# Rotary position in the retention heads: partners 64 features apart, sines multiplied across partitions on two engines

## The chip, the core and the metric

The kernel runs on one core of one Trainium2 chip. The metric is the device time of one execution in microseconds, of which the median of three is taken. The profile that is read here is one more execution, taken by the hardware profiler. TensorE (PE) does the matrix products, VectorE (DVE), ScalarE (ACT) and GpSimd (POOL) the elementwise work, and SyncE (SP) and ScalarE issue the transfers. Each engine works through its own instructions in the order in which the program lists them. An instruction that waits for another engine holds up all that stand behind it in its own queue.

## What is computed

One block of a diffusion transformer over 2048 tokens of 1024 features: a modulated norm, a mixer with four HGRN2 heads and four retention heads of 128 features each, an output projection, and a convolutional feed-forward part. The change touches the rotary position of the retention heads' queries and keys, before they enter the chunked retention scan. Cut to that:

```python
def _rope_2d(t, rows, cols):
    half = t.shape[-1] // 2
    quarter = half // 2
    freqs = ROPE_THETA ** (-jnp.arange(quarter, dtype=jnp.float32) / quarter)

    def rot(u, pos):
        ang = pos[:, None] * freqs[None, :]
        cos, sin = jnp.cos(ang), jnp.sin(ang)
        u1, u2 = u[..., :quarter], u[..., quarter:]
        return jnp.concatenate([u1 * cos - u2 * sin, u1 * sin + u2 * cos], axis=-1)

    return jnp.concatenate([rot(t[..., :half], rows), rot(t[..., half:], cols)], axis=-1)
...
    rq = _heads(rq, RET_HEADS)
    rk = _heads(rk, RET_HEADS) * (RET_DK ** -0.5)
    rv = _heads(rv, RET_HEADS)
    if pos is not None:
        rq = _rope_2d(rq, pos[0], pos[1])
        rk = _rope_2d(rk, pos[0], pos[1])
...
    def step(r, inp):
        qc, kc, vc = inp
        scores = jnp.einsum('bhtk,bhsk->bhts', qc, kc) * intra
        o = (jnp.einsum('bhts,bhsv->bhtv', scores, vc)
             + jnp.einsum('bhtk,bhkv->bhtv', qc * q_dec[:, :, None], r))
        r_new = (chunk_dec[:, None, None] * r
                 + jnp.einsum('bhsk,bhsv->bhkv', kc * k_dec[:, :, None], vc))
        return r_new, o
```

Each feature is multiplied by a cosine, and its partner, 32 features further on or back, by a sine with a sign; the two are added. The products of queries with keys do not depend on the order of a head's 128 features, as long as both have the same.

## The kernel before

The heads come one after the other, first the four HGRN2 heads, then the four retention heads, and each goes over the 2048 tokens in four groups of 512. While PE, DVE and ACT work on the scan of one group, the projections of the next are woven between (`weave`, `step`): `ret_proj` makes queries, keys and values of a group, `ret_sweep1` uses them a group later, and `ret_sweep2` and `ret_sweep2b` finish the group of the head before. There are thus 16 runs of `ret_proj`, four heads by four groups; they are called units 1 to 16 here, in order of time. They lie between about 740 and 1290 us of the span.

In `ret_proj` a tile `qk` holds queries and keys of the group, 128 features on the partitions and 2 x 512 tokens along each. It is written in pieces out of PSUM by DVE (L587) and last by ACT (L585, in the helper `scaled`), and it has the slots named K0 and K1, so that the profile shows it as K. A second tile of the same size, `pt`, shows as Q. Four transfers that ACT issues (L1169) copy `qk` into `pt` with blocks of 32 partitions swapped in pairs. GpSimd multiplies `pt` by the sines (L1189), DVE multiplies `qk` by the cosines in place (L1192) and adds `pt` to it (L1193). Between the copies and these lies the projection of values and gates (in the fourth head of values alone). The cosines' product is held back until the last combining addition of that projection (`issue_after`). The first to use the rotated tile is PE, with the products of keys and queries (L1202, `rsc`).

Three other chains run on the same queues. The norm of a finished group: ACT sums squares (L913), GpSimd makes the reciprocal root in six small steps (L67 to L72, `rstd`), DVE scales by it (L935, or L1243 in retention heads), and PE transposes the result (L920, `otp`). The rotary tables are loaded for each group by ACT's queue (L1159, cosines into a single buffer, sines into one of three). And the weights and the modulation are prepared a head ahead (L291, L489 to L498, L644, L645).

The order on every queue is set by a scheduler that goes by its own model of durations when the program is built. A change in what stands in `ret_proj` can therefore move its neighbours as well.

Of the kernel before, what the change touches and what calls it, by code (L numbers as in the profile page):

```python
# [15 lines left out]
ALU = mybir.AluOpType  # L16
PSUM = bass.MemoryType.PSUM

P = 128
# [3 lines left out]
G = 512  # L23
# [6 lines left out]
NIN = 4608  # L30
# [11 lines left out]
H = G // 2  # L42
RING = 10
SEQUENCE = 0, 1, 5, 6, 4, 3, 2


def view(t, off, dims):
    return bass.AP(t.tensor, t.offset + off, [t.ap[0]] + dims)


class Kern:
# [411 lines left out]

    def features(self, h, g, ms=SEQUENCE):

        if g in self.X:
            return self.X.pop(g)
        X = [None] * 7
        for m in ms:
            X[m] = self.slot_tile([P, 4, 2, H], F16, "hx", "hx")  # L470
            self.nc.sync.dma_start(X[m], self.hxd[g][m])
        return X
# [679 lines left out]
    def ret_proj(self, pool, h, g, W, pr, cur):  # L1152
        nc = self.nc
        X = self.features(NH + h, g)
        qk, pt = self.kq_tiles()
        cos = pool.tile([P, G], F32, tag="Ta", bufs=1, name="cos")
        sin = pool.tile([P, G], F32, tag="Kl", bufs=KL, name="sin")
        for i, r in enumerate((cos, sin)):
            nc.scalar.dma_start(r, self.I["rope"][:, i, g * G:(g + 1) * G])  # L1159
        w, dq = W["z"]  # L1160
        if "dqk" not in W:
            W["dqk"] = self.kp.tile([P, 1], F32, tag="dqk", bufs=2, name="dqk")
            nc.vector.tensor_scalar(W["dqk"], dq, P ** -0.5, None, ALU.mult)

        def kq(f, half, c, s):
            self.scaled(qk[:, 1 - f, half * H:(half + 1) * H], c, s, dq if f else W["dqk"])
        yield from self.head_unit(*self.fm(w, X, H), kq, (W["dqk"], dq))
        for b in range(4):
            nc.scalar.dma_start(pt[32 * b:32 * b + 32], qk[32 * (b ^ 1):32 * (b ^ 1) + 32])  # L1169
        V = pool.tile([P, 4, P], F32, tag="V", bufs=2, name="rV")  # L1170
        if h < NH - 1:
            w, dqv = W["vg"]
            gate = self.gate_tile().rearrange("p (c t) -> p c t", t=P)

            def vg(f, half, c, s):
                cs = slice(2 * half, 2 * half + 2)
                if f:
                    c = self.whole(c, s)
                    nc.scalar.activation(gate[:, cs], c, AF.Silu, scale=dqv)
                else:  # L1180
                    self.scaled(V[:, cs], c, s, dqv)
            yield from self.head_unit(*self.tm(w, X, H), vg, (dqv, None))
            self.silu_bound(h, g, gate)
            cur["sg"][g] = gate
        else:
            w, dqv = W["v"]
            yield from self.single(*self.tm(w, X, H), dqv, lambda half: V[:, 2 * half:2 * half + 2])

        nc.gpsimd.tensor_tensor(pt, pt, view(sin, 0, [[0, 2], [1, G]]), ALU.mult)  # L1189

        with self.tc.issue_after(self.last.ins):
            nc.vector.tensor_tensor(qk, qk, view(cos, 0, [[0, 2], [1, G]]), ALU.mult)  # L1192
        nc.vector.tensor_tensor(qk, qk, pt, ALU.add)  # L1193
        pr.update(qk=qk, V=V)
# [596 lines left out]
def _consts():  # L1791
    s = np.arange(P)
    masks = []
    for h in LEVELS:
        same = (s[:, None] // (2 * h)) == (s[None, :] // (2 * h))
        m = (same & ((s[:, None] // h) != (s[None, :] // h))).astype(np.float32)
        if 2 * h <= B:
            masks.append(np.concatenate([m[j:j + B, j:j + B] for j in range(0, P, B)], 0))
    masks = np.concatenate(masks, 1)
    f = s.astype(np.float32)  # L1800
    ramp = np.zeros((P, 4, P), np.float32)
    rel = f[None, :] - f[:, None]
    ramp[:, 0], ramp[:, 1] = np.maximum(rel, 0), np.maximum(-rel, 0)
    ramp[:, 2], ramp[:, 3] = rel >= 0, rel <= 0
    colr = np.stack([P - 1 - f, f, f + 1, P - f], 1).astype(np.float32)
    fr = (np.float32(10000.0) ** (-np.arange(32, dtype=np.float32) / np.float32(32))).astype(np.float32)
    pos = np.arange(64, dtype=np.float32)
    ang = (fr[s % 32][:, None] * pos[None, :]).astype(np.float32)
    sign = np.where((s % 64) < 32, -1.0, 1.0).astype(np.float32)

    tok = np.arange(SEQ)
    at = np.where((s < 64)[:, None], ang[:, tok // 64], ang[:, tok % 64])
    rope = np.stack([np.cos(at), np.sin(at) * sign[:, None]], 1).astype(np.float32)
    return dict(ident=np.eye(P, dtype=np.float32), masks=masks, ramp=ramp, colr=colr, rope=rope)

# [21 lines left out]
```

## Time and profile before

| | |
|---|---|
| three runs | 2725.51 us median (2723.41 to 2730.9) |
| the profiled execution | 2735.92 us, of it span 2734.1 us |
| PE busy | 2557.4 us, 94% of the span |
| DVE busy | 1821.8 us, 67% |
| ACT busy | 1343.0 us, 49% |
| POOL busy | 779.3 us, 29% |
| PE's mean granted clock | 0.969 of full speed |

Times inside the span are counted from its start. A gap is the time that an engine sat idle just before an instruction, and its releaser the instruction that ended the wait. PE is the busiest engine by far, so what counts is where PE sits idle and which chain of other engines it waits for there. A busy PE instruction takes longer at a lower granted clock, so gaps and clock have to be read together.

### The profile page before, as it was taken

Reading aid. Unit: us, or ns where it says so; the run is one execution under the profiler, and the core shown is the slowest. Engines: PE = TensorE matmul, PEld = TensorE weight load, DVE = VectorE, ACT = ScalarE, POOL = GpSimd, SP = SyncE. Lnnn points to the kernel's source line nnn. Section 1 sums busy time; section 2 is a strip of 40 time slices with the busy share of each in tenths; the row PEclk is TensorE's granted clock in tenths of the full one; section 3 lists DMA queues with packets and bytes.
Section 4 is the critical chain, followed back from the end, with each engine's and each line's share of the span. In section 5 each row is a group of like instructions: output and inputs, shape, how many; then the busy total and the mean of one; then the engine's idle time right before and its main releaser. Section 6 shows DMA issues by size and latency. Waiting matters only on the chain.

```text
span 2734.1 us, 56424 instructions
## 1 busy us (share of the span) xinstructions
PE 2557.4 (94%) x22829; PEld 1686.3 (62%) x22829; DVE 1821.8 (67%) x3569; ACT 1343.0 (49%) x2902; POOL 779.3 (29%) x905
## 2 busy tenths in 40 slices
PE   5788999999999999988999899999999999999998
PEld 2578888889888888887445344444444444444443
DVE  4988677776757565546464888877877777423553
ACT  4776456564544444435454566555555554411120
POOL 3733112220313132221244344334433433000101
PEclk6799999999999999999999999999999999999999
DMA  8224334243447676766631133333233234734552
GB/s 282 115 86 156 103 110 135 93 132 115 144 132 255 207 238 198 241 184 196 211 110 62 57 121 104 108 112 113 99 105 116 89 112 163 268 143 172 205 194 100
DMA packets 216694, 402.39 MB, mean 147 GB/s; under 512 B 16623, under 2 KB 98771, under 8 KB 211824
## 3 DMA queue, kind: packets, MB, share of 16 engines
q1 hardware_dynamic: 203808, 373.42, 39.8%
q10 hardware_dynamic: 12320, 25.18, 3.0%
q8 instruction: 179, 2.93, 0.4%
q14 instruction: 83, 0.68, 0.1%
q0 software_dynamic: 304, 0.17, 0.0%
HBM read 298.57 MB, written 91.75 MB: 143 GB/s over the span
## 4 chain that ended last, share of the span: by engine, by line
PE 61%; DVE 15%; DMA 8%; issue 7%; ACT 4%; POOL 4%; ACTq 1%; SPq 0%; POOLq 0%; DVEq 0%
PE pa L84 6%; PE pa L85 6%; PE pa L86 6%; PE pd L86 5%; PE pd L84 5%; PE pd L85 5%; DMA Q<-K 3%; PE pc L84 3%; PE pc L85 3%; PE pc L86 3%; PE pb L84 2%; PE pb L86 2%; PE pb L85 2%; PE opp L84 2%; PE opp L85 2%
## 5 line engine op out<-in xcount | busy, mean ns | idle before, releaser
L84 PE MATMUL pa<-feat,w 128*128 128x512 f16 x704 | 268.4, 381 | 14.2 <-ACT ta L545 9.8
L85 PE MATMUL pa<-feat,w 128*128 128x512 f16 x704 | 268.1, 381 | 0.0
L86 PE MATMUL pa<-feat,w 128*128 128x512 f16 x704 | 264.9, 381 | 0.0
L86 PE MATMUL pd<-wd,actl 128*128 128x512 f16 x616 | 233.5, 379 | 0.0
L85 PE MATMUL pd<-wd,actl 128*128 128x512 f16 x616 | 233.5, 379 | 0.0
L84 PE MATMUL pd<-wd,actl 128*128 128x512 f16 x616 | 232.8, 379 | 0.0
L85 PEld LDWEIGHTS <-w 128*128 128x128 f16 x1232 | 120.7, 98 | 156.8 <-issue 16.9
L86 PEld LDWEIGHTS <-w 128*128 128x128 f16 x1232 | 121.4, 99 | 145.3 <-issue 1.7
L84 PEld LDWEIGHTS <-w 128*128 128x128 f16 x1232 | 121.5, 99 | 141.4 <-issue 2.0
L85 PEld LDWEIGHTS <-hx 128*128 128x128 f16 x1824 | 182.0, 100 | 9.5 <-issue 7.3
L86 PEld LDWEIGHTS <-hx 128*128 128x128 f16 x1824 | 182.1, 100 | 2.8 <-issue 1.9
L84 PEld LDWEIGHTS <-hx 128*128 128x128 f16 x1824 | 182.4, 100 | 2.3
L1593 DVE SCALAR_TENSOR_TENSOR st<-act,modT,st 128x512 f16<-128x512 f32 x154 | 144.3, 967 | 32.1 <-ACT st L1592 32.1
L1592 ACT ACTIVATE st<-act,modT 128x512 f16<-128x512 f32 x154 | 107.3, 718 | 85.2 <-DVE act L1582 31.4
L84 PE MATMUL pa<-w_vg,hx 128*128 128x128 f16 x800 | 145.2, 222 | 2.9 <-DVE cb L579 2.3
L85 PE MATMUL pa<-w_vg,hx 128*128 128x128 f16 x800 | 144.9, 222 | 0.0
L86 PE MATMUL pa<-w_vg,hx 128*128 128x128 f16 x800 | 144.8, 222 | 0.0
L84 PE MATMUL pc<-feat,w 128*128 128x512 f16 x352 | 133.5, 379 | 1.2 <-ACT feat L1367 1.1
L86 PE MATMUL pc<-feat,w 128*128 128x512 f16 x352 | 133.5, 379 | 0.0
L85 PE MATMUL pc<-feat,w 128*128 128x512 f16 x352 | 133.5, 379 | 0.0
L84 PE MATMUL pa<-hx,w_z 128*128 128x256 f16 x464 | 127.7, 275 | 5.1 <-ACT ct L545 1.6
L85 PEld LDWEIGHTS <-w_z 128*128 128x128 f16 x1072 | 109.2, 102 | 36.4 <-issue 24.1
(550 smaller groups left out, 7563.0 us busy)
## 6 DMA issues: line engine op xcount, KB each, us to landing
hx<-hxd SPq DMA_DIRECT2D x212, 512.0 KB, 4.9
actd<-st SPq DMA_DIRECT2D x154, 256.0 KB, 2.0
actl<-actd SPq DMA_DIRECT2D x28, 1024.0 KB, 5.0
wur<-in_w_up_dram SPq DMA_DIRECT2D x44, 512.0 KB, 3.8
raw<-in_w_in_dram SPq DMA_DIRECT2D x36, 512.0 KB, 4.3
wm<-in_w_mod_dram SPq DMA_DIRECT2D x64, 256.0 KB, 3.8
hxd<-hx SPq DMA_DIRECT2D x28, 512.0 KB, 3.2
wdb<-in_w_down_dram SPq DMA_DIRECT2D x44, 256.0 KB, 4.0
```

The costliest lines, as they stand in the source:

```text
L84: mm(ps, lhs(0), rhs(0), start=start, stop=False, skip_group_check=True)
L85: mm(ps, lhs(0), rhs(1), start=False, stop=False, skip_group_check=True)
L86: mm(ps, lhs(1), rhs(0), start=False, stop=stop, skip_group_check=True)
L1592: nc.scalar.activation(p[:, 0], v, AF.Copy, scale=s)
L1593: nc.vector.scalar_tensor_tensor(p[:, 1], v, s, p[:, 0], ALU.mult, ALU.subtract)
```

## The change

The two columns of weights that make queries and keys of a retention head are put in another order on the way into the kernel, so that the partner of feature p lies at p + 64 or p - 64, and no longer 32 away in blocks. The cosine and sine tables are put in the same order. The four copies go. Instead GpSimd multiplies the lower 64 partitions of `qk` by the sines and writes the product to the upper 64 partitions of `pt`, and DVE does the other half, from the upper partitions to the lower. Both stand right behind the pieces of `qk`, before the projection of values and gates; GpSimd's product behind that projection goes. The sign of a sine now goes with the partition that is read. Cosines and addition stay as they were.

```diff
+HALVES = np.arange(P).reshape(2, 2, 32).transpose(1, 0, 2).reshape(P)
...
         yield from self.head_unit(*self.fm(w, X, H), kq, (W["dqk"], dq))
-        for b in range(4):
-            nc.scalar.dma_start(pt[32 * b:32 * b + 32], qk[32 * (b ^ 1):32 * (b ^ 1) + 32])
+        sines = view(sin, 0, [[0, 2], [1, G]])
+        nc.gpsimd.tensor_tensor(pt[64:], qk[:64], sines[:64], ALU.mult)
+        nc.vector.tensor_tensor(pt[:64], qk[64:], sines[64:], ALU.mult)
         V = pool.tile([P, 4, P], F32, tag="V", bufs=2, name="rV")
...
-        nc.gpsimd.tensor_tensor(pt, pt, view(sin, 0, [[0, 2], [1, G]]), ALU.mult)
         with self.tc.issue_after(self.last.ins):
             nc.vector.tensor_tensor(qk, qk, view(cos, 0, [[0, 2], [1, G]]), ALU.mult)
...
-    sign = np.where((s % 64) < 32, -1.0, 1.0).astype(np.float32)
+    sign = np.where(s < 64, 1.0, -1.0).astype(np.float32)
...
-    at = np.where((s < 64)[:, None], ang[:, tok // 64], ang[:, tok % 64])
+    at = np.where((HALVES < 64)[:, None], ang[HALVES][:, tok // 64], ang[HALVES][:, tok % 64])
...
+    order = np.arange(NIN)
+    for o in range(2560, 3584, P):
+        order[o:o + P] = o + HALVES
+    named["w_in"] = np.ascontiguousarray(named["w_in"][:, :, order])
```

The lines behind the change are four to six higher than before. Outside the retention heads and the first steps of the output projection the queues' order is as it was.

GpSimd's queue at units 3 and 4, whose two products stand next to each other ahead of a norm's six steps (L67 to L72, after: L71 to L76; raw is a weight tile). Before:

```order
L489 TENSOR_TENSOR raw<-raw 128x512
L492 TENSOR_TENSOR raw<-raw 128x512
L495 TENSOR_TENSOR raw<-raw 128x512
L498 TENSOR_TENSOR raw<-raw 128x512
L1189 TENSOR_TENSOR Q<-Q,sin 128x1024 x2
L67 TENSOR_SCALAR rs_v<-ossq 128x4
L68 TENSOR_TENSOR rs_y<-rs_v,mhalf 128x4
```

After:

```order
L493 TENSOR_TENSOR raw<-raw 128x512
L496 TENSOR_TENSOR raw<-raw 128x512
L499 TENSOR_TENSOR raw<-raw 128x512
L502 TENSOR_TENSOR raw<-raw 128x512
L1174 TENSOR_TENSOR Q<-K,sin 64x1024 x2
L71 TENSOR_SCALAR rs_v<-ossq 128x4
L72 TENSOR_TENSOR rs_y<-rs_v,mhalf 128x4
```

Nothing moved: the products stand in the same places, but read K in place of Q, and so wait for the pieces of `qk` and no longer for a transfer.

VectorE's queue at unit 7, from the last piece of `qk` that DVE writes (K<-pc) to a piece of the values (rV); w_z is a weight tile, modT the modulation. Before:

```order
L587 SCALAR_TENSOR_TENSOR K<-pc,dq,ct 128x256
L645 SCALAR_TENSOR_TENSOR w_z<-raw,p2s,w_z 128x512 x2
L235 TENSOR_TENSOR modT<-modt_ps,sv 128x4
L645 SCALAR_TENSOR_TENSOR w_z<-raw,p2s,w_z 128x512
L587 SCALAR_TENSOR_TENSOR rV<-pb,dq,ct 128x256
```

After:

```order
L591 SCALAR_TENSOR_TENSOR K<-pc,dq,ct 128x256
L649 SCALAR_TENSOR_TENSOR w_z<-raw,p2s,w_z 128x512 x2
L239 TENSOR_TENSOR modT<-modt_ps,sv 128x4
L1175 TENSOR_TENSOR Q<-K,sin 64x1024
L649 SCALAR_TENSOR_TENSOR w_z<-raw,p2s,w_z 128x512
L591 SCALAR_TENSOR_TENSOR rV<-pb,dq,ct 128x256
```

One instruction came in between weights that are being prepared; the rest kept its order.

VectorE's queue at unit 13, the first of the last head, from a group's state (Kt, Sf, rSb; ou is the finished group) to the rotated tile. Before:

```order
L1224 SCALAR_TENSOR_TENSOR rSb<-Kt,cd,rup 128x128
L903 SCALAR_TENSOR_TENSOR ou<-Sf,cd,ou 128x128
L903 SCALAR_TENSOR_TENSOR ou<-ou,cd 128x128 x2
L631 SCALAR_TENSOR_TENSOR rV<-pb,dq,cs 128x256
L1228 SCALAR_TENSOR_TENSOR ou<-rob,qd,ou 128x512
L1236 SCALAR_TENSOR_TENSOR ou<-o_18272,qd,ou 128x512
L1192 TENSOR_TENSOR K<-K,cos 128x1024
L1193 TENSOR_TENSOR K<-K,Q 128x1024
```

After:

```order
L1175 TENSOR_TENSOR Q<-K,sin 64x1024
L1229 SCALAR_TENSOR_TENSOR Kt<-Kt,cd,rup 128x128
L907 SCALAR_TENSOR_TENSOR Sf<-ou,cd 128x128
L1229 SCALAR_TENSOR_TENSOR rSb<-Kt,cd,rup 128x128
L907 SCALAR_TENSOR_TENSOR ou<-Sf,cd,ou 128x128
L1197 TENSOR_TENSOR K<-K,cos 128x1024
L635 SCALAR_TENSOR_TENSOR rV<-pb,dq,cs 128x256
L907 SCALAR_TENSOR_TENSOR ou<-ou,cd 128x128
L1233 SCALAR_TENSOR_TENSOR ou<-rob,qd,ou 128x512
```

The cosines' product moved up, ahead of the values' piece and of the finished group, and the sines' product stands four instructions ahead of it.

## Rows read from the trace of the kernel before

**Rows 1.** Busy time of each engine in the stretch of the rotary units: us, PE, PEld, DVE, ACT and POOL busy (x instructions), mean granted clock of PE, DMA share, GB/s.

```profile
760.00:1290.00 530.00, 478.52 (x5819) 449.75 (x5816) 318.26 (x694) 237.35 (x597) 122.22 (x144) 0.96 0.65 210
```

**Rows 2.** What PE waited for in 740 to 1300 us, two of the first lines: who waited for whom, us in total, times, longest us.

```profile
PE otp L920 <- DVE ou L1243: 12.9, 4, 6.7
PE rsc L1202 <- DVE K L1193: 7.8, 3, 3.2
```

**Rows 3.** The line of the four copies, L1169: duration ns min/median/max, first and last start us; who waited for it (us, times); time from issue to landing.

```profile
L1169 ACTq DMA_DIRECT2D Q<-K x64: 513/554/1306, 769.8 to 1244.5; - x64
...
  POOL Q L1189: 215.6, 14
  DVE K L1192: 20.5, 8
...
DMA to landing us min/median/max: 2.3/4.9/8.5
```

**Rows 4.** Ten instructions of PE in order of time within three kinds (timeline of PE: start us, us, what [gap before it <-releaser]): the transpose of a finished group at units 2, 4, 5, 8 and 9, the products of keys and queries at units 7, 11, 13 and 16, and a product of the context's keys in unit 13.

```profile
820.63 0.55 PE L920 MATMUL otp<-ident,ou 128*128 128x128 f32 x3 [1.49 <-DVE ou L935]
...
881.99 0.88 PE L920 MATMUL otp<-ident,ou 128*128 128x128 f32 x3 [2.54 <-DVE ou L935]
...
916.52 0.87 PE L920 MATMUL otp<-ident,ou 128*128 128x128 f32 x3 [2.98 <-DVE ou L935]
...
1009.22 0.30 PE L920 MATMUL otp<-ident,ou 128*128 128x128 f32 x1 [1.65 <-DVE ou L1243]
...
1046.95 0.85 PE L920 MATMUL otp<-ident,ou 128*128 128x128 f32 x3 [3.36 <-DVE ou L1243]
...
983.77 0.70 PE L1202 MATMUL rsc<-K 128*128 128x128 f32 x2 [3.13 <-DVE K L1193]
...
1110.80 0.80 PE L1202 MATMUL rsc<-K 128*128 128x128 f32 x2 [3.16 <-DVE K L1193]
...
1173.36 0.80 PE L1202 MATMUL rsc<-K 128*128 128x128 f32 x2 [1.53 <-DVE K L1193]
...
1257.78 0.79 PE L1202 MATMUL rsc<-K 128*128 128x128 f32 x2 [4.52 <-DVE p2t L97]
...
1170.97 0.22 PE L84 MATMUL pa<-hc,w_z 128*128 128x128 f16 x1 [4.33 <-ACT cs L625]
```

**Rows 5.** The cosines' product on DVE in units 7, 11, 13 and 16, and behind the first of them its addition (timeline of DVE).

```profile
979.03 1.23 DVE L1192 TENSOR_TENSOR K<-K,cos 128x1024 f32<-128x1024 f32 x1 [1.89 <-DMA Q<-K]
982.49 1.22 DVE L1193 TENSOR_TENSOR K<-K,Q 128x1024 f32<-128x1024 f32 x1 [2.23 <-POOL Q L1189]
...
1106.06 1.23 DVE L1192 TENSOR_TENSOR K<-K,cos 128x1024 f32<-128x1024 f32 x1 [1.92 <-DMA Q<-K]
...
1168.62 1.23 DVE L1192 TENSOR_TENSOR K<-K,cos 128x1024 f32<-128x1024 f32 x1 [5.78 <-DMA Q<-K]
...
1253.05 1.23 DVE L1192 TENSOR_TENSOR K<-K,cos 128x1024 f32<-128x1024 f32 x1 [4.54 <-DMA Q<-K]
```

**Rows 6.** GpSimd in unit 4: the sines' product, and the first and last step of the norm behind it (timeline of POOL).

```profile
876.26 2.36 POOL L1189 TENSOR_TENSOR Q<-Q,sin 128x1024 f32<-128x1024 f32 x1 [22.75 <-DMA Q<-K]
878.71 0.19 POOL L67 TENSOR_SCALAR rs_v<-ossq 128x4 f32<-128x4 f32 x1
...
880.92 0.20 POOL L72 TENSOR_TENSOR rs_y<-rs_y,rs_t 128x4 f32<-128x4 f32 x1
```

**Rows 7.** ACT in unit 4: the last piece of `qk`, and the last sum of squares of that norm (timeline of ACT).

```profile
866.14 0.47 ACT L585 ACTIVATE K<-pa,dqk 128x256 f32<-128x256 f32 x1 [5.02 <-DMA wm<-in_w_mod_dram]
...
875.35 0.19 ACT L913 ACTIVATION_READ_ACCUMULATOR qf<-ou 128x1 f32 x1
```

**Rows 8.** ACT in unit 13 ahead of the context's keys: the load of the next cosines, and the square behind it (timeline of ACT; ACTq is its queue of transfers).

```profile
1169.87 0.34 ACTq L1159 DMA_DIRECT2D cos<-in_rope_dram  x1
1170.26 0.31 ACT L913 ACTIVATE qf<-ou 128x128 f32<-128x128 f32 x1 [5.85 <-DVE K L1192]
```

**Rows 9.** The three rotary instructions in 740 to 1300 us, by line: count | busy us, mean ns | idle before us <-releasers.

```profile
L1189 POOL TENSOR_TENSOR Q<-Q,sin 128x1024 f32<-128x1024 f32 x16 | 46.8, 2928 | 232.9 <-DMA Q<-K 215.6 <-DMA mixd<-qf 8.7 <-DVE Sf L903 8.5
...
L1192 DVE TENSOR_TENSOR K<-K,cos 128x1024 f32<-128x1024 f32 x16 | 22.5, 1406 | 20.6 <-DMA Q<-K 20.5
L1193 DVE TENSOR_TENSOR K<-K,Q 128x1024 f32<-128x1024 f32 x16 | 21.3, 1331 | 14.4 <-POOL Q L1189 14.3
```

**Rows 10.** Two ACT copies of 128 elements along each partition, one of 128 partitions and one of 32, by line and shape (columns as in rows 9).

```profile
L774 ACT COPY cs<-rup 128x128 f32<-128x128 f32 x8 | 2.1, 265 | 3.5 <-PE rup L1120 1.5 <-DVE Sf L903 1.0 <-DVE cs L775 0.8
L854 ACT COPY A<-sf 32x128 f32<-32x128 f32 x8 | 2.0, 253 | 0.1
```

**Rows 11.** Unit 3: the sines' product on POOL and the cosines' on DVE at the same time (timelines of POOL and of DVE).

```profile
851.16 2.35 POOL L1189 TENSOR_TENSOR Q<-Q,sin 128x1024 f32<-128x1024 f32 x1 [7.10 <-DMA Q<-K]
...
851.39 3.21 DVE L1192 TENSOR_TENSOR K<-K,cos 128x1024 f32<-128x1024 f32 x1
```

**Rows 12.** Six stretches in which the granted clock was 0.50, the first of them and the sum of all (columns as in rows 1; the sum names PE, PEld, DVE, ACT and POOL).

```profile
881.50:884.90 3.40, 2.91 (x24) 2.88 (x25) 3.40 (x5) 2.66 (x7) 1.91 (x2) 0.50 0.48 164
...
sum 34.00, PE 29.67 PEld 26.49 DVE 24.26 ACT 13.91 POOL 7.41; mean PE 4.95 PEld 4.42 DVE 4.04 ACT 2.32 POOL 1.24
```

**Rows 13.** ACT in unit 13: the load of its sines and the last piece of its `qk` (timeline of ACT), and below them the line of all these loads, L1159, from issue to landing.

```profile
1144.03 0.33 ACTq L1159 DMA_DIRECT2D sin<-in_rope_dram  x1
...
1156.89 0.51 ACT L585 ACTIVATE K<-pa,dqk 128x256 f32<-128x256 f32 x1
...
DMA to landing us min/median/max: 2.5/5.2/9.1
```

## The prediction

> **What bounds the kernel now.** I read the busy time by stage first. In the 530 us in which the sixteen rotary units lie, PE works for 478.52 us, so 51.5 us are all that any change here can win while PE's work stays the same, apart from the clock. VectorE is busy for 318.26 us, 60%, and GpSimd for 122.22 [rows 1]. Then the waits of PE: two of its longest lines end at the transpose of a finished group and at the products of keys and queries [rows 2]. The line of the copies shows who hangs on them: GpSimd for 215.6 us and VectorE for 20.5 [rows 3]. Most of GpSimd's wait costs nothing, since it has little else to do. The question is which of PE's gaps end a chain that begins at the copies. I went through PE's gaps of over 1.4 us one by one and followed each back. Ten of them do [rows 4].
>
> Four stand before the products of keys and queries. In unit 7 VectorE was free 1.89 us before its cosine product, which waited for the copies to have read their source; then it waited 2.23 us for GpSimd's sines [rows 5]. Only after the addition could PE go on, 3.13 us late [rows 4].
>
> Five stand before the transpose of a finished group, and here the copies act by GpSimd's queue. In unit 4 the last piece of the queries and keys was there at 866.14 + 0.47 = 866.6, the sine product began at 876.26, and the norm's first step stood behind it until 878.71, though its sums of squares were complete at 875.35 + 0.19 = 875.5 [rows 6, 7]. It started 3.2 us late, and PE lost 2.54 us [rows 4].
>
> The tenth is in unit 13. ACT's load of the next cosines came out only at 1169.87, when the cosine product had given its buffer back, and ACT's squares behind it had waited 5.85 us [rows 8]. PE's product of the context's keys came 4.33 us late [rows 4].
>
> **What goes.** The copies with their issue, 64 x 0.554 = 35 us of ACT's queue, and their landing, 4.9 us in the median [rows 3]. ACT is busy less than half of this stage [rows 1], so its 35 us I count at nothing beyond the ten gaps; if that is wrong it is a further gain.
>
> Without copies the sine products can begin when the last piece is there. In unit 4 that is 9.6 us sooner [rows 6, 7]. Even the slower form of the product, 3.4 us, then ends at 870.0, before the squares do. The five transposes then wait for their own norm alone: 1.49 + 2.54 + 2.98 + 1.65 + 3.36 = 12.0 us [rows 4].
>
> The cosine product then starts when VectorE is free: 1.89, 1.92, 5.78 and 4.54 us sooner in the four units, and the addition right behind it, without the 2.23 us [rows 5]. In unit 7 that is 977.14 + 1.23 + 1.22 = 979.6, and with a sine product of 1.22 us pushed in ahead on VectorE 980.8. PE was ready at 983.77 - 3.13 = 980.64 [rows 4], so at most 0.2 us are left. Units 13 and 16 have 2 us and more in hand by the same sum, unit 11 comes out as unit 7. I take all four: 3.13 + 3.16 + 1.53 + 4.52 = 12.3 us. The 4.33 us in unit 13 go with them. Together 12.0 + 12.3 + 4.3 = **28.7 us of gaps**.
>
> **The clock.** Behind six of these gaps the granted clock stood at 0.50, which is 1.2 of 2.4 GHz, after PE had idled for 2.54 to 4.52 us [rows 4]. PE was busy for 29.67 us in these stretches [rows 12]. At full clock the same work would take half as long, 14.8 us less. That is the upper bound; below it is 0, where another chain is late in the same microseconds. I take half, **7.4 us**, since other gaps stay in this stage and a dip may follow them in turn.
>
> **What comes.** On VectorE 16 sine products. The nearest row is the cosine product, 128 partitions by 1024 elements, which takes 1.22 us where nothing is in its way [rows 5]. With half the partitions it is hardly shorter: an ACT copy of 32 partitions takes 253 ns against 265 for 128 [rows 10]. So I take 1.22; below stands half of it, above the 3.21 us of a product that met GpSimd's [rows 11]. 16 x 1.22 = 19.5 us (9.8 to 51). VectorE is busy 60% of this stage [rows 1], and in the other 40% a product runs in time that would be idle. So 0.60 x 19.5 = **11.7 us** delay what stands behind, and I count them as if PE waited for every one, which is on the cautious side.
>
> On GpSimd 16 products stay, on half the partitions, still with 1024 elements each. Before they took 2.35 to 3.4 us, 2.93 in the mean [rows 6, 9], and I leave that. What no row shows is an engine that writes to other partitions than it reads. Below, the price is half of 2.35; above I set the whole chain that it replaces, from the last piece to the product's end, 878.6 - 866.6 = 12 us [rows 6, 7], at which nothing is won. I take 2.93, the row of the same instruction, because nothing in it but the partitions changes.
>
> New waits. The cosines now wait for GpSimd to have read its half. Where the projection of values and gates lies between, that is over before their turn comes. In units 13 to 16 few instructions lie between, and the cosines can wait for up to one sine product of 2.35 us; behind them stand a piece of the values and a finished group. They waited 5.78 and 4.54 us for the copies in units 13 and 16 [rows 5], so it is a smaller wait in the same place. VectorE's sine product waits for ACT's last piece of the queries and keys; behind it in unit 7 are weights that nobody needs soon. And both products need the sines earlier than GpSimd did. In unit 13 they were issued at 1144.03, and the pieces were there at 1157.4: 13 us, against a slowest landing of 9.1 [rows 13], so no new wait. The copies' traffic, 64 transfers in a stage whose transfer engines are 0.65 busy [rows 1], leaves room for the others; no gap of PE here ends at a transfer, so I count nothing.
>
> **The sum.** 28.7 + 7.4 - 11.7 = 24.4 us less in the profiled execution, which took 2735.9 and lies 10.4 above the median of the runs. Since the gaps are no part of that difference that I can name, the same amount is taken off the median: 2725.5 - 24.4 = **2701**. At its best, 28.7 + 14.8 and no cost on PE, it would be 2682; at its worst, 28.7 - 19.5 with no gain from the clock, 2716. That is the forecast's own range.
>
> **The rivals.** *Something else is late next.* The scheduler set every queue in this stage anew, and the norm's squares on ACT, or VectorE's own queue, may end a microsecond after the copies did. For it: squares and copies lay 3 us apart in unit 4 [rows 6, 7], and PE's order assumed both in time. Against it: in all four products of keys and queries VectorE was demonstrably free before the copies came [rows 5]. If only these 12.3 us go and the 11.7 us come, the time is 2725, between 2717 and 2733.
>
> *The two engines stand in each other's way, and it gets slower.* In unit 3 GpSimd's product began at 851.16 and took 2.35 us; VectorE's began at 851.39 and ended at 854.60, 1.1 us after GpSimd's, where it takes 1.22 alone [rows 11]. So VectorE did its work after GpSimd, not beside it. Before the change such a meeting fell on a VectorE that was waiting for the same copies anyway; now GpSimd starts right behind the pieces, in the middle of VectorE's other work. The price is 16 x (1.22 + 2.35) = 57 us of VectorE. If PE sees four fifths of that, 45.7, the time is 2725.5 - 28.7 + 45.7 = 2742; it turns slower from a share of one half. Against it: VectorE is idle 40% of the stage, and its sine product wakes on the same piece as GpSimd's and may well go first.
> The Trainium skill says the same (SBUF — State Buffer, "Who interferes with whom"): a VectorE instruction with two inputs in SBUF and a GpSimd instruction that reads SBUF exclude each other for a whole instruction, and whoever starts first wins. By that rule the two sine products never run side by side, and GpSimd's may hold up any two-input instruction of VectorE; the trace agrees in unit 3.
>
> *Crossing the partitions is dear, and the change does not do what it says.* If GpSimd's product takes 10 us and more, the norm behind it is as late as before, the cosines wait for it, and VectorE's additional work is left: 2725.5 + 11.7 = 2737 at the most, 2725 where it only just replaces the copies. For it stands only that no row shows such a write.
>
> **How the numbers follow.** Forecast 0.70, something else late 0.13, in each other's way 0.11, dear crossing 0.06 (half of it within 0.3%). A difference of 0.3%, 8.2 us, is about what a measurement of this kernel can tell from none. So faster 0.70, the same 0.13 + 0.03 = 0.16, slower 0.11 + 0.03 = 0.14. The range runs from 2678, a little under the best case since ACT's freed queue is not in it, to 2728, which takes in most of the second case; some 0.16 lie above it, and 0.04 below.
>
> **What the profile after would show.** No copies on ACT, and GpSimd's sine product within a microsecond of the last piece of the queries and keys, at 2.4 to 3.5 us. The ten gaps gone or under a microsecond, PE's idle time in the stage down from 51 us to between 25 and 35, and fewer stretches at clock 0.50. VectorE some 20 us busier. The forecast is wrong if PE waits as long as before for finished groups or rotated tiles, with GpSimd's product or VectorE's queue as the releaser, or if GpSimd's product takes over 8 us.

## The result, and the profile after

The changed kernel takes 2700.5 us (median of four runs, 2698.62 to 2701.94), the kernel before 2724.46 on the same chip. The ratio is 0.9913 [0.9893, 0.9933]. A second measurement of it gave 2699.77 and 0.9901 [0.9888, 0.9915]. The forecast was 2701.

The whole difference lies in the rotary stage. I take it from the end of PE's wait for `sf` near 750 us to the first product of the output projection, since its length is what changed. One window over it (columns as in [rows 1]), of before:

```profile
751.60:1296.90 545.30, 489.89 (x5926) 459.74 (x5927) 327.54 (x717) 245.17 (x615) 125.31 (x151) 0.96 0.64 207
```

And of after:

```profile
749.00:1261.80 512.80, 478.44 (x5926) 453.13 (x5927) 354.49 (x733) 246.18 (x615) 129.64 (x151) 0.98 0.61 204
```

PE does the same 5926 products in 32.5 us less. Length less PE's busy time is PE's idle time: 55.4 us before, 34.4 after, so 21 us are gaps. The other 11.4 us are PE's own busy time, and here the clock shows: 0.96 became 0.98. VectorE is 27 us busier. In the two spans, 2734.1 and 2699.5 us, all but 2 us of the difference lie in this stage.

The rotary instructions by line and shape, 740 to 1300 us (columns as in [rows 9]; L1174 and L1175 are the two sine products, L1197 and L1198 cosines and addition):

```profile
L1174 POOL TENSOR_TENSOR Q<-K,sin 64x1024 f32<-64x1024 f32 x16 | 50.4, 3150 | 163.3 <-ACT K L589 163.0
...
L1175 DVE TENSOR_TENSOR Q<-K,sin 64x1024 f32<-64x1024 f32 x16 | 25.8, 1614 | 9.9 <-ACT K L589 9.6
L1197 DVE TENSOR_TENSOR K<-K,cos 128x1024 f32<-128x1024 f32 x16 | 21.4, 1336 | 0.0
L1198 DVE TENSOR_TENSOR K<-K,Q 128x1024 f32<-128x1024 f32 x16 | 21.3, 1329 | 0.1
```

Cosines and addition waited 20.6 and 14.4 us [rows 9]; they now wait for nothing. GpSimd's product waits for the last piece of `qk`, and it starts within 0.2 us of it in thirteen units, 0.8 us after it in unit 3, and 2.3 us after it in units 7 and 11, where GpSimd is still preparing weights. In unit 4 that piece and the product, then the last square of the norm's sums and the norm's first step (timelines of ACT and POOL):

```profile
857.55 0.47 ACT L589 ACTIVATE K<-pa,dqk 128x256 f32<-128x256 f32 x1 [4.74 <-PE pa L90]
...
858.11 3.40 POOL L1174 TENSOR_TENSOR Q<-K,sin 64x1024 f32<-64x1024 f32 x1 [16.63 <-ACT K L589]
...
866.76 0.19 ACT L917 ACTIVATION_READ_ACCUMULATOR qf<-ou 128x1 f32 x1
...
867.11 0.44 POOL L71 TENSOR_SCALAR rs_v<-ossq 128x4 f32<-128x4 f32 x1 [5.61 <-ACT qf L917]
```

The product begins 0.1 us after the piece (857.55 + 0.47 = 858.02) and is over 5.6 us before the norm needs GpSimd. In [rows 6, 7] 9.6 us lay between piece and product. Of PE's waits in 740 to 1300 us (columns as in [rows 2]):

```profile
PE otp L924 <- DVE ou L1248: 9.9, 3, 7.1
PE sf L844 <- DVE Q L853: 4.4, 2, 2.8
PE pa L88 <- DVE rV L591: 4.1, 2, 2.1
PE modt_ps L236 <- DVE macc L295: 3.8, 2, 2.0
```

None of the ten gaps of [rows 4] is left; at PE's products of keys and queries in units 4 and 8, two other places, 0.73 and 0.71 us remain. The 7.1 us before `otp` come after the last unit and were there before, with 6.7 us [rows 2]. Two waits have grown: `pa` behind `rV` from 0.5 to 4.1 us, `modt_ps` behind `macc` from 1.8 to 3.8. Two transposes of finished groups near the end, at 1211.63 and 1232.38, are late by 1.60 and 2.31 us. The first is as late or later in two of the experiments below, by 1.60 us in e3 and 2.09 in e5; their cause is not shown. Half of the wait for `macc` belongs to unit 5, half to unit 9. In unit 5 (timelines of DVE, POOL and PE):

```profile
889.00 0.75 DVE L295 SCALAR_TENSOR_TENSOR macc<-wm,silc,macc 128x512 f32<-128x512 f32 x1 [1.92 <-DMA wm<-in_w_mod_dram]
889.79 1.22 DVE L1175 TENSOR_TENSOR Q<-K,sin 64x1024 f32<-64x1024 f32 x1
891.05 2.72 DVE L295 SCALAR_TENSOR_TENSOR macc<-wm,silc,macc 128x512 f32<-128x512 f32 x1
...
889.89 3.33 POOL L1174 TENSOR_TENSOR Q<-K,sin 64x1024 f32<-64x1024 f32 x1 [10.95 <-ACT K L589]
...
893.82 1.05 PE L236 MATMUL modt_ps<-ones,macc 128*128 128x1 f32 x8 [2.01 <-DVE macc L295]
```

Both engines wake on the same piece, VectorE first. GpSimd's product, 2.35 us when alone [rows 6], takes 3.33. The sum of modulations behind VectorE's product, two inputs in SBUF, takes 2.72 us instead of 0.75, and ends half a microsecond after GpSimd's product (893.8 against 893.2). PE waits 2.01 us for it. In unit 7 GpSimd comes later, but what stands behind VectorE's product is held up by it in the same way (timelines of DVE, POOL and PE):

```profile
956.03 2.11 DVE L1175 TENSOR_TENSOR Q<-K,sin 64x1024 f32<-64x1024 f32 x1
958.17 2.73 DVE L649 SCALAR_TENSOR_TENSOR w_z<-raw,p2s,w_z 128x512 f16<-128x512 f32 x1
960.83 0.47 DVE L591 SCALAR_TENSOR_TENSOR rV<-pb,dq,ct 128x256 f32<-128x256 f32 x1
...
957.14 3.21 POOL L1174 TENSOR_TENSOR Q<-K,sin 64x1024 f32<-64x1024 f32 x1
...
961.35 0.27 PE L88 MATMUL pa<-hx,w_z 128*128 128x256 f16 x1 [1.96 <-DVE rV L591]
```

PE's product behind that `rV` came 1.96 us late. So the second rival's mechanism is there, at a smaller price.

### The profile page after: what moved, and what is told of

It is laid out like the page before. It is cut to its first block, busy times and chain, and to the rows that moved or that the text cites. A ratio compares the mean times of both kernels' runs of the same rounds, so it can differ in the third digit from the quotient of the medians.

```text
span 2699.5 us, 56351 instructions
## 1 busy us (share of the span) xinstructions
PE 2544.2 (94%) x22829; PEld 1680.0 (62%) x22829; DVE 1847.7 (68%) x3585; ACT 1344.8 (50%) x2902; POOL 785.0 (29%) x905
## 4 chain that ended last, share of the span: by engine, by line
PE 71%; DVE 15%; ACT 4%; issue 4%; DMA 3%; POOL 2%; SPq 0%; DVEq 0%; ACTq 0%; POOLq 0%
PE pa L88 8%; PE pa L89 8%; PE pa L90 8%; PE pd L89 5%; PE pd L90 5%; PE pd L88 5%; PE pc L88 4%; PE pc L89 4%; PE pc L90 4%; PE pb L88 2%; PE pb L90 2%; PE pb L89 2%; PE opp L89 2%; PE opp L88 2%; PE opp L90 2%
## 5 line engine op out<-in xcount | busy, mean ns | idle before, releaser
L88 PE MATMUL pa<-hx,w_z 128*128 128x256 f16 x464 | 127.6, 275 | 7.5 <-DVE rV L591 4.1
L89 PE MATMUL pa<-hx,w_z 128*128 128x256 f16 x464 | 127.3, 274 | 0.0
```

Source lines behind the costliest of these rows:

```text
L88: mm(ps, lhs(0), rhs(0), start=start, stop=False, skip_group_check=True)
L89: mm(ps, lhs(0), rhs(1), start=False, stop=False, skip_group_check=True)
```

## Experiments

Each series was timed on one chip, beside the kernel before: e1 to e4, then e5, e6 and the two kernels again, then e7 and e9, then e10 and e11. The table has the medians, the ratios to the kernel before, and the stage as above. "At 1.2 GHz" is the time within it at the lower granted clock, by the trace's clock records.

| kernel | us | ratio [95%] | stage | PE idle | PE busy | at 1.2 GHz |
|---|---|---|---|---|---|---|
| before, first profile | 2724.46 | | 545.3 | 55.4 | 489.9 | 46.8 |
| before, again (b2) | 2729.69 | 1.0008 [0.9997, 1.0018] | 535.9 | 50.5 | 485.4 | 34.2 |
| after, first profile | 2700.5 | 0.9913 [0.9893, 0.9933] | 512.8 | 34.4 | 478.4 | 24.6 |
| after, again (a2) | 2699.77 | 0.9901 [0.9888, 0.9915] | 509.8 | 32.9 | 476.9 | 21.7 |
| both halves on GpSimd (e1) | 2692.67 | 0.9874 [0.9859, 0.9889] | 503.4 | 29.5 | 473.9 | 11.9 |
| both on VectorE (e2) | 2693.38 | 0.9877 [0.9863, 0.9890] | 505.3 | 29.4 | 475.9 | 22.6 |
| VectorE's half later (e3) | 2693.49 | 0.9877 [0.9864, 0.9891] | 501.6 | 26.9 | 474.8 | 19.0 |
| both on VectorE, later (e9) | 2697.2 | 0.9886 [0.9867, 0.9905] | 509.2 | 30.3 | 478.9 | 27.7 |
| before, sines on VectorE (e4) | 2719.14 | 0.9969 [0.9959, 0.9979] | 529.0 | 45.1 | 483.9 | 40.9 |
| before without copies (e5) | 2689.34 | 0.9867 [0.9854, 0.9880] | 498.1 | 27.0 | 471.1 | 11.6 |
| after + 128 dead transfers, ACT (e6) | 2738.59 | 1.0043 [1.0030, 1.0056] | 543.2 | 60.9 | 482.2 | 27.8 |
| after + 64 dead transfers, ACT (e7) | 2731.88 | 1.0008 [0.9993, 1.0024] | 532.5 | 47.4 | 485.1 | 41.0 |
| after + 64 dead transfers, SP (e11) | 2713.3 | 0.9938 [0.9921, 0.9954] | 523.9 | 39.8 | 484.1 | 35.8 |
| before, copies issued by SP (e10) | 2726.44 | 0.9996 [0.9986, 1.0006] | 532.6 | 49.0 | 483.6 | 32.9 |

### Where the sine products run

Both halves on GpSimd.

```diff
-        nc.vector.tensor_tensor(pt[:64], qk[64:], sines[64:], ALU.mult)
+        nc.gpsimd.tensor_tensor(pt[:64], qk[64:], sines[64:], ALU.mult)
```

> Both halves of the sine product on GpSimd, as two instructions one behind the other; VectorE makes none. Theory: what VectorE's half costs is not its 1.22 us but the place, where VectorE's queue stands still until ACT's last piece of the queries and keys is there; with it six gaps of PE of 1.3 to 2.1 us, 10.6 us in all, should go, and GpSimd's 4.7 us still end before the norm's squares are complete: 5 to 11 us under the changed kernel, 2690 to 2696. Rival, the shared use of the two engines: GpSimd now stands in VectorE's way for twice as long, and the time is that of the changed kernel or more, 2700 to 2710.

It took 2692.67 us, where its theory had 2690 to 2696. Of the six gaps that the expectation counts, the waits for `macc` in units 5 and 9 and for `rV` in units 7 and 11 are gone; the two before `pc` stay, with 1.56 and 1.47 us, and one of 1.73 us behind `rV` came near 845 us. The run can't tell its two explanations apart, since it takes away VectorE's stand behind ACT's last piece and the meeting of the two products at once.

Both halves on VectorE.

```diff
-        nc.gpsimd.tensor_tensor(pt[64:], qk[:64], sines[:64], ALU.mult)
+        nc.vector.tensor_tensor(pt[64:], qk[:64], sines[:64], ALU.mult)
```

> Both halves of the sine product on VectorE, none on GpSimd. Theory: VectorE's queue stands still at the first half as before, the second adds 1.22 us where the queue is busy, so 0 to 6 us over the changed kernel, 2700 to 2707. Rival, the two engines in each other's way: without GpSimd's product nothing of VectorE's is held up, and the time falls under the changed kernel's, 2690 to 2697.

2693.38 us: the theory, by which VectorE's work itself costs, missed, and the rival hit. The same place as above (timelines of DVE and PE):

```profile
889.06 1.22 DVE L1174 TENSOR_TENSOR Q<-K,sin 64x1024 f32<-64x1024 f32 x1 [0.18 <-ACT K L589]
890.29 1.22 DVE L1175 TENSOR_TENSOR Q<-K,sin 64x1024 f32<-64x1024 f32 x1
891.55 0.75 DVE L295 SCALAR_TENSOR_TENSOR macc<-wm,silc,macc 128x512 f32<-128x512 f32 x1
...
892.35 0.49 PE L236 MATMUL modt_ps<-ones,macc 128*128 128x1 f32 x3 [0.43 <-DVE macc L295]
```

VectorE has twice the sine work here, and is through with it and with `macc` in 889.06 to 892.30, 3.2 us. In the changed kernel half that work and `macc` took from 889.79 to 893.77, 4.0 us. PE's gap falls from 2.01 to 0.43. This run tells the explanations apart: VectorE still waits for ACT's last piece, 9.2 us in all against 9.6, and GpSimd's product is gone. At the four places PE waits 3.4 us in place of 7.9; 1.21 and 1.30 of it are the waits for `rV`.

VectorE's half later, right ahead of the cosines.

```diff
-        nc.vector.tensor_tensor(pt[:64], qk[64:], sines[64:], ALU.mult)
...
         with self.tc.issue_after(self.last.ins):
+            nc.vector.tensor_tensor(pt[:64], qk[64:], sines[64:], ALU.mult)
```

> As the changed kernel, but VectorE's half stands behind the projection of values and gates, right ahead of the cosines, and GpSimd's stays early. Theory: VectorE's queue no longer stands still for ACT's last piece, so the six gaps of 10.6 us shrink; the rotated tile comes 1.22 us later, which up to four units feel: 0 to 8 us under the changed kernel, 2692 to 2700. Rival: the place of VectorE's half is indifferent and only its 19.5 us count: 2700, within 3.

2693.49 us, within its theory's 2692 to 2700. The division of work is that of the changed kernel; the meeting is taken apart, and VectorE's stand behind ACT's last piece goes with it.

Both halves on VectorE, right ahead of the cosines.

```diff
-        nc.gpsimd.tensor_tensor(pt[64:], qk[:64], sines[:64], ALU.mult)
-        nc.vector.tensor_tensor(pt[:64], qk[64:], sines[64:], ALU.mult)
...
         with self.tc.issue_after(self.last.ins):
+            nc.vector.tensor_tensor(pt[64:], qk[:64], sines[:64], ALU.mult)
+            nc.vector.tensor_tensor(pt[:64], qk[64:], sines[64:], ALU.mult)
```

> Both halves on VectorE and both behind the projection, right ahead of the cosines. Theory, that VectorE's half costs where it makes one long stand with GpSimd's behind the last piece of the queries and keys: no such stand here, but the rotated tile comes 2.4 us later: 2689 to 2698, as the three variants before it. Rival, that VectorE's work counts by its amount: 2698 to 2705.

2697.2 us. Its interval holds both the changed kernel's ratio in the second measurement and those of the three above, so it tells nothing apart. Its one profile, of the slowest of its four runs, has a stage of 509.2 us, as long as that of a2, with less idle time (30.3 us against 32.9) and more time at 1.2 GHz (27.7 against 21.7).

### What the copies cost

The kernel before with its sine product on VectorE; the copies stay.

```diff
-        nc.gpsimd.tensor_tensor(pt, pt, view(sin, 0, [[0, 2], [1, G]]), ALU.mult)
+        nc.vector.tensor_tensor(pt, pt, view(sin, 0, [[0, 2], [1, G]]), ALU.mult)
```

> The kernel before, copies and all, but its one sine product of 128 partitions is made by VectorE and no longer by GpSimd. Theory: GpSimd's queue is no longer held by the copies, so the five late transposes of finished groups (12.0 us) come in time, while the rotated tile is still late by the copies, less the wait for GpSimd: 10 to 18 us under the kernel before, 2707 to 2715. Rival: the transposes were late by something else than GpSimd's queue, and nothing moves: 2720 to 2728.

2719.14 us, 7 less, where 11 to 19 were expected. Of the five gaps before the transposes those of units 2, 4 and 5 went, to 0.23 us or nothing. Those of units 8 and 9 stayed, with 2.68 us (1.65 before) and 1.84 (3.36), since VectorE's queue now stands where GpSimd's stood. In unit 8 (timelines of DVE and PE):

```profile
999.95 1.23 DVE L1189 TENSOR_TENSOR Q<-Q,sin 128x1024 f32<-128x1024 f32 x1 [4.08 <-DMA Q<-K]
...
1001.85 0.30 PE L920 MATMUL otp<-ident,ou 128*128 128x128 f32 x1 [2.68 <-DVE ou L1243]
```

The scaling of the finished group stood behind that product. Other gaps came, at 1156.10 with 3.66 us before a product of keys and queries. Here the late input was not cured by another reader.

The kernel before without copies. The sine product reads `qk` in place of its exchanged copy, so the exchange of partners is left out.

```diff
-        for b in range(4):
-            nc.scalar.dma_start(pt[32 * b:32 * b + 32], qk[32 * (b ^ 1):32 * (b ^ 1) + 32])
...
-        nc.gpsimd.tensor_tensor(pt, pt, view(sin, 0, [[0, 2], [1, G]]), ALU.mult)
+        nc.gpsimd.tensor_tensor(pt, qk, view(sin, 0, [[0, 2], [1, G]]), ALU.mult)
```

> The kernel before without its four copies: GpSimd multiplies the queries and keys themselves by the sines, all 128 partitions, in the old line behind the projection. The exchange of the partners is left out, so this is the transfer's price alone, without a product on VectorE and without a write across partitions. Theory, that the late copies made all ten gaps and that VectorE's half beside GpSimd's costs some 8 us: 2686 to 2694, under the changed kernel by as much. Rival, that the gain came with the products' new place and the new order of the queues: 2705 to 2720.

2689.34 us. Against the kernel before in the same series (b2) the stage is 37.8 us shorter: 23.5 of PE's idle time and 14.3 of its busy time. From here to the changed kernel of that series (a2) it is 11.7 us longer, 5.9 idle and 5.8 busy: the price of the new division, together with the products' new place, which this pair does not separate from it.

The two kernels again, unchanged, in that series.

> The kernel before once more, for a second profiled execution. The first took 2735.9 us, some 10 over the median of its runs. If those 10 us lay in the stage of the rotary units, that stage takes 535 to 540 us here in place of 545; if they lay elsewhere, it takes 545 again. Its time 2720 to 2731.

> The changed kernel once more, beside the others of this call: 2698 to 2703, and the stage of the rotary units 513 us as in its first profile, within 3.

The medians lie 0.2% and 0.03% from the first ones. The stage of the changed kernel came out 3.0 us shorter than in its first profile, 509.8 against 512.8. That of before came out 9.4 shorter: it took 535.9 us where the first profile had 545.3. At the ten places of [rows 4] PE idles for 1.48, 2.95, 3.06 and 0.71 us before four of the transposes and not at all before the fifth, for 2.01, 3.17, 0.95 and 2.68 before keys and queries, and for 4.28 in unit 13. These are 21.3 us, where the first profile had 28.7. Two of them, units 2 and 8 (timeline of PE):

```profile
817.53 0.33 PE L920 MATMUL otp<-ident,ou 128*128 128x128 f32 x1 [1.48 <-DVE ou L935]
...
1001.75 0.30 PE L920 MATMUL otp<-ident,ou 128*128 128x128 f32 x1 [0.71 <-DVE ou L1243]
```

In these two profiles the same program loses a different amount at the copies.

### Is it the copies' lateness, or ScalarE's queue?

The changed kernel with 128 transfers of 64 KB on ScalarE's queue that nobody reads, into one scratch tile.

```diff
+        scr = pool.tile([P, G], F32, tag="scr", bufs=1, name="scr")
+        for b in range(8):
+            nc.scalar.dma_start(scr[32 * (b % 4):32 * (b % 4) + 32], sin[32 * (b % 4 ^ 1):32 * (b % 4 ^ 1) + 32])
```

> The changed kernel, and with it 128 further transfers of 64 KB that ACT issues behind each unit's sine products, from the sines to a scratch tile that nobody reads: the traffic of the copies and twice their number of issues, but no wait. Theory, that the copies cost by their lateness and not by ACT's queue or their traffic: the changed kernel's time within 4 us, 2698 to 2705. Rival, that a third or more of the gain is ACT's freed queue and the transfer engines' room: 2709 or more.

2738.59 us, slower than the kernel before, though no instruction uses what they move. Two of ACT's waits (740 to 1300 us):

```profile
ACT ct L551 <- DMA scr<-sin: 26.4, 5, 6.3
...
ACT qf L917 <- DMA scr<-sin: 11.4, 4, 6.3
```

A transfer to a tile that an earlier one still writes stands in ACT's queue until that has landed, and ACT's pieces and squares stand behind it. That is a wait that the copies of before did not have, so I gave each transfer a place of its own in main memory, and took 64 of 128 KB, the copies' number and size.

```diff
+        self.deadd = [dp.tile([P, 2, G], F32, name=f"dead{k}") for k in range(4 * NG)]
...
+        for b in range(4):
+            nc.scalar.dma_start(self.deadd[h * NG + g][32 * b:32 * b + 32], view(sin[32 * b:32 * b + 32], 0, [[0, 2], [1, G]]))
```

> The changed kernel with four dead transfers of 128 KB per unit on ACT's queue, behind the unit's sine products, from the sines to a region of HBM of their own that nobody reads: as many issues as the four copies, half of the run before with dead transfers, and no two of them into the same place. In that run ACT issued for 69 us and stood still for some 38 more, and it cost 39 us. Theory now, that ACT's queue is a price of the copies besides their lateness: 64 issues, 35 us, at the same rate 0.36 of it, 2708 to 2718. Rival, that only the waits among the transfers into one scratch tile cost: 2698 to 2705.

2731.88 us (2718.77 to 2742.02 in 12 runs): both expectations missed. ACT's waits still name them:

```profile
ACT ct L552 <- DMA dead<-sin: 8.6, 2, 6.0
...
ACT cb L552 <- DMA dead<-sin: 6.2, 1, 6.2
...
ACT gate L1188 <- DMA dead<-sin: 5.5, 1, 5.5
```

The same 64 transfers issued by SyncE:

```diff
-            nc.scalar.dma_start(self.deadd[h * NG + g][32 * b:32 * b + 32], view(sin[32 * b:32 * b + 32], 0, [[0, 2], [1, G]]))
+            nc.sync.dma_start(self.deadd[h * NG + g][32 * b:32 * b + 32], view(sin[32 * b:32 * b + 32], 0, [[0, 2], [1, G]]))
```

> The changed kernel with the same 64 transfers of 128 KB that nobody reads (the sines of each unit, written to main memory, each to a place of its own) as in the run that had them on ScalarE's queue, now issued by SyncE. Theory 'what cost there was ScalarE's queue, by the issue and the waits in it': the time is that of the changed kernel, 2697 to 2707, and the stretch behind the rotary units is as long as there (1438 us). Rival 'the traffic itself costs': 2722 to 2738 as on ScalarE's queue, with the clock or gaps behind loads as the place.

2713.3 us, between the two expectations. Against a2 the medians give 32.1 us for e7 and 13.5 for this run; by the ratios, each to the kernel before of its own series, they are 29 and 10. So 10 to 14 us come with these transfers even from SyncE, and 19 more with ScalarE as the issuer. Of those 19 only about half lie where the transfers are issued: in the two profiles the stage is 8.6 us shorter here (523.9 against 532.5), and the stretch behind it, in which no such transfer is issued, 9.4 us (1440.6 against 1450.0). ACT's waits for the transfers are down from 20.3 to 2.1 us.

Last the real copies, issued by SyncE in the kernel before.

```diff
-            nc.scalar.dma_start(pt[32 * b:32 * b + 32], qk[32 * (b ^ 1):32 * (b ^ 1) + 32])
+            nc.sync.dma_start(pt[32 * b:32 * b + 32], qk[32 * (b ^ 1):32 * (b ^ 1) + 32])
```

> The kernel before, with the four copies of a unit issued by SyncE instead of ScalarE; their data, their readers and their number are the same. Theory 'the copies come late, whoever issues them': GpSimd's sines, and the norm behind them, start as long after the last piece as before (some 5 us of flight), so most of the ten gaps stay; 2718 to 2732 us, within 0.3% of the kernel before. Rival 'what costs is ScalarE's queue': with 64 issues of 0.55 us and their waits gone from ScalarE, most of the gain of the kernel without copies comes at once, 2695 to 2710. Also possible, and against both: the wait for a piece of qk now stands in SyncE's queue and holds up the weights that it loads; then over 2735, with gaps of PE that end at a load.

2726.44 us, 0.9996 [0.9986, 1.0006]: ScalarE's queue is free of them and nothing is won. The copies land 4.1 us after their issue in the median, hardly sooner than the 4.9 of [rows 3], and waits behind them stay. But they are at other places than expected: of the ten gaps only 6.4 us are left, 3.25 and 1.59 of it before the transposes of units 9 and 4, and PE's idle time is 49.0 us all the same, since others came. GpSimd's product and the norm behind it in unit 9, and the way through the cosines in unit 7 (timelines of POOL, DVE, ACT and PE):

```profile
1028.43 2.35 POOL L1189 TENSOR_TENSOR Q<-Q,sin 128x1024 f32<-128x1024 f32 x1 [18.19 <-DMA Q<-K]
1030.86 0.19 POOL L67 TENSOR_SCALAR rs_v<-ossq 128x4 f32<-128x4 f32 x1
...
1033.80 0.30 PE L920 MATMUL otp<-ident,ou 128*128 128x128 f32 x1 [3.25 <-DVE ou L1243]
...
973.03 1.23 DVE L1192 TENSOR_TENSOR K<-K,cos 128x1024 f32<-128x1024 f32 x1 [3.98 <-DMA wm<-in_w_mod_dram]
...
974.85 0.33 ACTq L1159 DMA_DIRECT2D cos<-in_rope_dram  x1
975.23 0.47 ACT L585 ACTIVATE rV<-pa,dq 128x256 f32<-128x256 f32 x1 [4.88 <-DVE K L1192]
...
975.76 0.27 PE L84 MATMUL pc<-hx,w_z 128*128 128x256 f16 x1 [3.20 <-ACT rV L585]
```

The norm's squares were done at 1026.76 and its first step began at 1030.86, 4.1 us late behind the sines. In unit 7 the cosines' product is late, the load of the next cosines stands in ACT's queue until its buffer is free, and the piece `rV` behind that: the tenth gap's chain, in another unit. The releaser that the row of the cosines' product names is a load of modulation weights, which the product does not read; in unit 11 the same product waits 3.84 us for the copies, and they have 14.1 us of its line's total. The other new gaps (4.56, 3.36 and 3.30 us are the longest) were not followed to their start. So the third case in the expectation, held-up weights, is not excluded: SyncE's queue stood 13.9 us at the longest for a piece of `qk`.

## Why the prediction came out

The time was right, but in part by luck: two sizes were wrong and cancelled, the gaps in the base too large and the clock too small, and a third, VectorE's half, came out for another reason than the one given.

**The gaps** (28.7 us). All ten went, as the prediction followed them: the sines right behind the piece, the norm on time, cosines and addition without a wait. From the first profile of before to the kernel without copies PE's idle time fell by 55.4 - 27.0 = 28.4 us; from the second, by 23.5. These are net sums over the stage, some small gaps elsewhere having come and gone.

**The clock** (7.4 us, bound 14.8). This term was too small. Without the copies PE's busy time fell by 489.9 - 471.1 = 18.8 us (from b2 by 14.3). The time at 1.2 GHz fell by 46.8 - 11.6 = 35.2 us, and half of that, 17.6, is what the same products save at full clock. The six stretches of [rows 12] were a part of it; the bound was a sum over those dips that followed a counted gap, 34 us of 46.8. That other gaps would start new dips was the reason for taking half. It holds for the changed kernel, with 24.6 us left, less for e1 and e5, with 12.

**VectorE's half** (11.7 us lost). The size came out, 11.7 us in the stage from e5 to a2, 14.7 to the first profile of after. The reason given, that each microsecond of new work on VectorE delays what stands behind by its busy share, is refuted, so the size is luck: e2 puts both halves there, 39 us of work, for which that rule asks 23, and is 6.4 us faster than the changed kernel. What is shown of the cost is that GpSimd's product holds up what stands right behind VectorE's. e1, e2 and e3 each take the meeting away in another manner and all come to 2692.7 to 2693.5; their intervals lie clear of the changed kernel's first one, and overlap its second by 0.0001 to 0.0003. e2 alone tells it from VectorE's wait for the piece; e9, which takes the meeting away as well, came to 2697.2 and confirms nothing. The prediction had this mechanism as its second rival, with 57 us of VectorE and four fifths of them on PE. In the changed kernel PE waits for it in four of the sixteen units: 2.01 and 1.84 us for `macc`, 1.96 and 2.10 for `rV`, 7.9 in sum, of which 3.4 remain in e2. Without the meeting the stage is 4.5 to 8.2 us shorter than in a2 (e1 to e3), and the time 6 to 7. The stages of e1 to e3 are still 3.5 to 7.2 us longer than that of e5, and where this rest comes from is not shown. About half of the 11.7 is the clock, 21.7 us at 1.2 GHz in a2 against 11.6 in e5.
The Trainium skill (SBUF — State Buffer, "Who interferes with whom") has the rule: two-input work of VectorE and a reading GpSimd exclude each other for a whole instruction. The trace agrees: 2.72 us instead of 0.75, and 3.33 instead of 2.35.

**ScalarE's freed queue** (counted at nothing). The copies cost the same when SyncE issues them, but at other gaps, so a gain of ScalarE's queue may be hidden by what SyncE's lost; the zero is not shown. Nor is it a general zero: 64 transfers that nobody needs cost 10 to 14 us from SyncE and some 30 from ScalarE, 12 of these 30 behind the stage. The findings fit if the copies' lateness hid what ScalarE's queue lost; that is argued, not shown. How the gain divides between the copies' lateness, which the ten gaps show, and their traffic and issue is therefore open.

**The base.** The prediction took 24.4 us off the median because it could name no part of the gaps in the 10.4 us by which the profile lay above it. The second profile of before names them: it has 7.4 us less at the ten places, and a stage 9.4 us shorter. So the base was too large by what the gaps of that one profile had above those of the second, and the clock term too small. Within one profile the account reads 28.4 + 18.8 - 14.7 = 32.5 us (545.3 to 498.1 to 512.8), where the prediction had 28.7 + 7.4 - 11.7 = 24.4; between the medians it is 24.0 in the first series and 28.6 in the second (from 2728.41, the median of all runs of the kernel before in that series).

**The signs named ahead** are there: the product within a microsecond of its piece in fourteen units (2.3 us in two) and 3.15 us long in the mean, PE's idle time at 34.4, in the range of 25 to 35, and 24.6 us at 1.2 GHz in place of 46.8. VectorE is 27 us busier, not 20: its sine products take 25.8 us in place of 19.5, since an instruction that is held up counts as busy.

**Crossing the partitions** costs nothing. VectorE's product takes 1.22 us, GpSimd's 2.35 at the least, as when they wrote to the partitions that they read. The third rival is out. The first, something else late next, showed only as far as the meeting goes, and perhaps in the two late transposes near the end: in unit 4 the squares ended 5.4 us after the product, and the other norms' first steps followed their squares within 0.7 us.

**Open** is where e7's stretch behind the stage comes from: from the first product of the output projection to the end it took 1450.0 us against 1438.1 in a2, and its runs are spread over 23 us. e10 has some of it, 1446.6 against 1440.1 in b2. No transfer of theirs is issued there. Both show the same PE gaps in the feed-forward part, near 1528, 1596 and 1603 us (2.08, 2.46 and 3.81 us in e7), where a2, b2 and e11 have others; PE's idle time there is 33.9 and 33.3 us, against 27.4 in a2 and 28.5 in b2. What sets them off is not shown.

## What to carry over

An instruction that waits for a transfer costs by what stands behind it in its queue; follow such a queue to the engine that sets the end before counting the transfer itself. When a product is divided between VectorE and GpSimd, look at what stands right behind VectorE's half while GpSimd works on the other: one engine for both, or VectorE's half later, was worth 6 to 7 us here (both on VectorE and later 2.6, within the noise). And before summing gaps of one profile, look at a second one of the same program: here the second had a quarter less.

## What was not expected of the hardware

Products that write to the other half of the partitions ran as fast as in place: 64 x 1024 elements in 1.22 us on VectorE (128 x 1024 in 1.23), and in 2.35 on GpSimd.

Transfers whose data nobody uses are not free: 64 of 128 KB, 8.4 MB beside 394, lengthened the program by 10 to 14 us from SyncE's queue, with PE 14.1 us longer at 1.2 GHz in the stage (35.8 against 21.7), and by some 30 from ScalarE's, 12 of them behind the stage and unexplained.

PE's clock carried two fifths of what the gaps cost: from the kernel before to the one without copies the stage fell by 28.4 us of idle time and 18.8 us of the same products' busy time.
